# The first feed-forward layer's scale made on TensorE: its weights move past a column of silu(c)

## The chip, the cores and the metric

The kernel runs on one core of one Trainium2 chip. The metric is the time of one execution on the device in microseconds (us). A core has TensorE (PE in the rows; PEld is its weight load), VectorE (DVE), ScalarE (ACT), GpSimd (POOL) and SyncE (SP, which issues the DMAs).

## The reference

Two models of two layers each run one after the other on a sequence of 256 tokens of width 1024. In the first one every layer has a mixer (attention with compressed keys and values in layer 0, a state-space mixer in layer 1) and a feed-forward part, and both are modulated by a vector `c` of 1024 values:

```python
cs = silu(c)                                    # [1, 1024]
for i in range(2):
    shift, scale, gate = split(cs @ mod_mix_w[i] + mod_mix_b[i], 3)   # w: [1024, 3072]
    h = x * (1 + scale) + shift
    y = mla_mixer(h, ...) if i == 0 else s5_mixer(h, ...)
    x = layer_norm(ALPHA * x + (1 + gate) * y)
    shift, scale, gate = split(cs @ mod_ffn_w[i] + mod_ffn_b[i], 3)
    h = x * (1 + scale) + shift
    y = mlp(h, ...)
    x = layer_norm(ALPHA * x + (1 + gate) * y)
```

There are four such products with a vector, of three thirds with 1024 results each. The change concerns one of the twelve: `scale` of the feed-forward part of layer 0. The second model has no modulation.

## The kernel before

All instructions of an engine are issued in the order in which the program writes them. The weights come as *units* of 128x1024 f32 (0.5 MB), in an order that `plan()` writes out by hand and that is the list `UNITS`. SP loads a unit into one of seven buffers `raw0` to `raw6` as soon as the unit seven places earlier is through. A unit of kind "w" is a matrix weight: ScalarE rounds it to f32r (`wh`, L464) and VectorE makes the remainder (`wl`, L504); both are kept in a ring of 11 places. A unit of kind "p" (tiles `early`) goes to a place of its own and is used by TensorE as it is, in f32. A unit of kind "m" is a piece of a modulation. `run()` handles the next units of the list, at most so many as the call says; calls of it are strewn by hand among the instructions of a stage.

A third of a modulation is named `mod<i><third>`: i = 0 mixer of layer 0, 1 feed-forward of layer 0, 2 and 3 the same of layer 1; third 0 is shift, 1 is scale, 2 is gate. It has eight units. In each of them the weights are laid out transposed, with 128 results on the partitions and 1024 inputs along a row. `mod_unit` has VectorE multiply the tile with `cs` (silu(c), broadcast to all partitions in the setup) and sum along the row (L555: a weighted sum into one column of `msum`; the product itself goes to the scratch tile `junk`). After the eighth unit VectorE adds the bias (L564), which gives the 128x8 columns `mcol`.

In layer 0 the attention comes first. Ahead of its loop over the heads stand, in this order on TensorE: the key projection (`kvk`), the value projection (`kvv`: stationary `gate`'s storage, 128x512 results, records `bank<-early,gate`), and query pair 0 (records `bank<-gate,early`, 128x256, sixteen of them). An f32 matmul appears in the profile as two records. VectorE rotates the pair (L1227 to L1229), and the loop `heads` follows, ten rounds in the order

```python
HEADS0 = "T2 S0 B0 1 A2 E0 1 N0 q 1"
```

In round i: T turns the probabilities of head i-2 (TensorE L1094, ScalarE copy L1095), S makes the scores of head i (TensorE), B their maximum (VectorE L1284), A attends for head i-2 (TensorE `bank<-z,z`, then ScalarE and VectorE split the result into `hh` and `hl`, L636 and L637), E is the exponential (ScalarE L1289), N the normalisation (VectorE L1295, ScalarE L1298), q in rounds 0, 2 and 4 the next query pair, and each 1 is a `run` of one unit. The units of `mod11` (the third in question) are taken in this stretch: units 0 and 1 ahead of query pair 0 (one before the value projection, one after it), 2 and 3 in round 0, 4 and 5 in round 1, 6 and 7 in round 2; with one "w" unit of the output projection in each round. The gate's third `mod02` follows in rounds 3 to 6, on VectorE. After the loop `need_mod("mod02")` makes the gate's rows (TensorE `bank<-ident,gcol`), and the output projection (`mla_o`, records `bank<-wh,hh`) begins.

GpSimd computes tables for the state-space mixer during the whole loop. PSUM has eight banks, handed out and returned in a queue (`bank()`, `rel()`).

Of the kernel before, what the change touches and what calls it, by code (L numbers as in the profile page):

```python
# [11 lines left out]
F32 = mybir.dt.float32  # L12
F32R = mybir.dt.float32r
I32 = mybir.dt.int32
AF = mybir.ActivationFunctionType
OP = mybir.AluOpType
# [34 lines left out]
    return [("w", tag, k) for k in range(n)]  # L51


def _mod(i, third):
    return [("m", "mod%d%d" % (i, third), k) for k in range(8)]


def _ffn_order(tag, nt, first, pair):
# [64 lines left out]
def _unit(inp, kind, tag, k, out):  # L123
# [3 lines left out]
    def col(w):  # L127
        out[:] = w[:, 128 * k:128 * k + 128].reshape(8, 128, 128).transpose(1, 0, 2).reshape(128, 1024)

    if kind == "m":  # L130
        i, third = int(tag[3]), int(tag[4])
        nm, l = _MOD[i]
        o = 1024 * third + 128 * k
        out[:] = inp[nm + "_w"][l][:, o:o + 128].T
        return
    if tag[:3] in _FFN:
        nm, l = _FFN[tag[:3]]
# [58 lines left out]


def _cols_spec():
    s = [("dsk", lambda i: i["ssm_d"][0])]
    for m, (nm, l) in _MOD.items():  # L200
        s.append(("modb%d" % m, lambda i, nm=nm, l=l: i[nm + "_b"][l]))
    for nm in ("ln_mix", "ln_ffn"):
        for l in range(2):
            for gb in "gb":
                key = "%s_%s" % (nm, gb)
                s.append((key + str(l), lambda i, key=key, l=l: i[key][l]))
    s.append(("qn", lambda i: i["mla_q_norm"][0]))
    s.append(("kn", lambda i: i["mla_kv_norm"][0]))
    for l in range(2):
        s.append(("b1%d" % l, lambda i, l=l: i["mlp_b1"][l]))  # L210
    s.append(("bglu", lambda i: i["ssm_b_glu"][0]))
    s.append(("lbin", lambda i: i["lru_b_in_2"][0]))
    for t in range(4):
        s.append(("cw%d" % t, lambda i, t=t: i["lru_conv_w_2"][0][t]))
    s.append(("cb", lambda i: i["lru_conv_b_2"][0]))
    s.append(("lbr", lambda i: i["lru_b_r_2"][0]))
    s.append(("lbi", lambda i: i["lru_b_i_2"][0]))
    s.append(("lam", lambda i: i["lru_lambda_2"][0]))
    s.append(("cb2", lambda i: i["lru_lambda_2"][0]))
    return s  # L220
# [17 lines left out]
UNITS = plan()  # L238
# [4 lines left out]
WPOS, RPOS = [0], [0]  # L243
for _u in UNITS:
    WPOS.append(WPOS[-1] + (_u[0] == "w"))
    RPOS.append(RPOS[-1] + (_u[0] in "mwx"))
RUNITS = [_j for _j, _u in enumerate(UNITS) if _u[0] in "mwx"]
SPARE = [(WPOS[UNITS.index(("w", "ssm_in", 7)) + 1] + _k) % RING for _k in SPARES]
PUNITS = [("p", "mla_in", _k) for _k in range(4)] + [("p", "kvk", 0), ("p", "kvv", 0)] + [("p", "qb", _k) for _k in range(4)]

# [62 lines left out]
class Model:  # L313
    def __init__(self, ctx, tc, ws, cols, rows, x, pos, inv, rel, sp, sbc, sgb, out):
# [31 lines left out]
        self.cs = T("cs", [128, 1024])  # L346
        self.msum, self.gcol = T("msum", [128, 8]), T("gcol", [128, 8])
        self.mhalf = T("mhalf", [128, 4])
        self.one = T("one", [128, 1])
        self.lri = T("lri", [128, 8], I32)  # L350
        self.banks = [ps.tile([128, 512], F32, name="bank%d" % i) for i in range(8)]
# [79 lines left out]
    def run(self, look=LOOK, maxn=99, mods=2):  # L431
        n = 0
        while self.nproc < len(UNITS) and n < maxn:
            i = self.nproc
            u = UNITS[i]
            if WPOS[i] > WPOS[self.ntake] + look:
                break
            if u[0] == "m":
                if mods == 0 or (self.hold and self.modfin is not None and u[1][4] == '2'):
                    break  # L440
                mods -= 1
# [6 lines left out]
            if u[0] == "w":  # L448
                nw = self.nw
                while self.rt and nw % RING in SPARE:  # L450
                    nw += 1
                s = nw % RING
                own = self.slot_owner[s]
                if own is not None and own not in self.finished:
                    break
                if own is None and not self.lent.get(s, set()) <= self.finished:
                    break
                if self.Hs[s] is None:
                    self.Hs[s], self.Ls[s] = (self.sb.tile([128, 1024], F32R, name="w%s%d_%d" % (c, s, i), tag="w%s%d" % (c, s))
                                              for c in "hl")  # L460
                self.nw = nw + 1
                self.slot_owner[s] = u
                self.slot_of[u] = s
                self.nc.scalar.activation(self.Hs[s], raw, func=AF.Copy)  # L464
                if u[1:] in POOLED:
                    for q in range(4):
                        w = slice(256 * q, 256 * q + 256)
                        self.nc.gpsimd.tensor_tensor(self.Ls[s][:, w], raw[:, w], self.f32(self.Hs[s])[:, w], op=OP.subtract)  # L468
                else:
                    self.plo.append((raw, s))  # L470
                    if not self.lag:
                        self.rests()
            elif u[0] == "m":
                self.mod_unit(u, raw)
            elif u[0] == "x":
                self.kept[u] = raw
            self.nproc += 1
# [67 lines left out]
    def mod_unit(self, u, raw):  # L545
# [16 lines left out]
        if k == 7:  # L562
# [3 lines left out]
            else:  # L566
                nc.vector.tensor_tensor(self.gcol, self.msum, self.col("modb%d" % i, 16, 8), op=OP.add)
                nc.vector.tensor_scalar(self.gcol, self.gcol, 1.0, None, op0=OP.add)
                self.modfin = [tag, 3]

    def mod_finish(self):
        if self.modfin is None:
            return
        self.mods.add(self.modfin[0])
        self.modfin = None
        for n in range(2):
            b = self.bank()
            for m in range(4):
# [403 lines left out]
    def setup(self):  # L982
# [28 lines left out]
        for n in range(2):  # L1011
            t = self.Z[0][:, 1024 + 512 * n:1536 + 512 * n]
            nc.scalar.activation(t, cb[n], func=AF.Tanh)
            V.scalar_tensor_tensor(self.cs[:, 512 * n:512 * n + 512], t, 1.0, cb[n], op0=OP.add, op1=OP.mult)
        self.rel(*cb)
        self.ssm_decay(spt, pi)
        posf = self.posf = self.stat(2)
        V.tensor_copy(posf, posi)
# [1092 lines left out]
```

## Time and profile before

| | us |
|---|---|
| median of 3 runs | 1686.18 (1681.76 to 1689.4) |
| profiled execution | 1684.43 |
| its span | 1682.7 |
| TensorE busy in the span | 1586.5 |
| VectorE busy in the span | 1129.5 |

The span is the time from the first to the last instruction of the profiled execution; the execution's own time is 1.7 us longer. A busy time counts an engine as busy while an instruction of it is recorded; TensorE's weight loads are counted apart. The granted clock (PEclk) is the share of its full speed that TensorE was given in a stretch.

### The profile page before, as it was taken

The numbers are of one execution on the slowest core, as the hardware profiler recorded it, in microseconds if no ns is written. First come the engines' busy times: TensorE is split into PE (matmuls) and PEld (weight loads), VectorE is DVE, ScalarE is ACT, GpSimd is POOL, SyncE is SP. The second block draws the span as 40 slices with busy tenths as digits, with TensorE's granted clock in tenths as the row PEclk, the third lists the DMA queues.
The fourth block names the chain that finished last, engine by engine and source line by source line (L and its number), as shares of the span: only waits on it lengthen the run. The fifth ranks groups of instructions, "written<-read, shape, count | busy, mean of one in ns | idle before, by whom it ended". The sixth has DMA issues, their size and how long they took to land.

```text
span 1682.7 us, 24904 instructions
## 1 busy us (share of the span) xinstructions
PE 1586.5 (94%) x9594; PEld 1398.7 (83%) x9594; DVE 1129.5 (67%) x1568; ACT 841.1 (50%) x1287; POOL 237.7 (14%) x309
## 2 busy tenths in 40 slices
PE   5879989998789999999999999999999999999998
PEld 2558888987778899789997779999899998779997
DVE  7877897779977755776554876555755555675553
ACT  3454567746355655354444855443644444664441
POOL 7990000013523000100000020000000001330000
PEclk9879999998889999999999999999999999999999
DMA  9774788968466565375551747564555653545540
GB/s 360 295 251 166 256 302 288 341 231 298 163 225 247 213 226 197 141 259 205 192 176 46 245 143 252 175 238 162 210 177 180 226 199 107 179 165 202 196 151 26
DMA packets 106586, 349.62 MB, mean 208 GB/s; under 512 B 12385, under 2 KB 22753, under 8 KB 106466
## 3 DMA queue, kind: packets, MB, share of 16 engines
q1 hardware_dynamic: 106466, 348.02, 59.1%
q8 instruction: 75, 1.23, 0.3%
q14 instruction: 45, 0.37, 0.1%
HBM read 338.41 MB, written 9.57 MB: 207 GB/s over the span
## 4 chain that ended last, share of the span: by engine, by line
PE 49%; DVE 4%; ACT 3%; issue 1%; POOL 1%; DMA 0%; DVEq 0%; POOLq 0%; ACTq 0%
PE bank L400 48%; ACT junka L693 1%; DVE wl L504 1%; PE bank L644 1%; ACT wh L464 0%; DMA raw<-in_ws_dram 0%; DVE r L731 0%; POOL wl L468 0%; DVE z L1844 0%; POOL st L689 0%; DVE z L1300 0%; DVE z L1910 0%; ACT r L1870 0%; DVE st L1284 0%; ACT z L1871 0%
## 5 line engine op out<-in xcount | busy, mean ns | idle before, releaser
L504 DVE TENSOR_TENSOR wl<-raw,wh 128x1024 fp32r<-128x1024 f32 x448 | 540.1, 1240 | 163.3 <-ACT wh L464 157.7
L464 ACT ACTIVATE wh<-raw 128x1024 fp32r<-128x1024 f32 x464 | 471.5, 1051 | 246.1 <-PE bank L400 141.9
L400 PE MATMUL bank<-xh,wh 128*128 128x256 f32 x1664 | 469.1, 282 | 0.0
L400 PE MATMUL bank<-xh,wl 128*128 128x256 f32 x1664 | 468.3, 281 | 0.0
L400 PE MATMUL bank<-xl,wh 128*128 128x256 f32 x1664 | 468.1, 281 | 0.0
L400 PEld LDWEIGHTS bank<-xh,wh 128*128 128x128 f32 x1664 | 317.0, 190 | 2.7 <-DVE z L1651 0.2
L400 PEld LDWEIGHTS bank<-xl,wh 128*128 128x128 f32 x1664 | 317.0, 190 | 2.1
L400 PEld LDWEIGHTS bank<-xh,wl 128*128 128x128 f32 x1664 | 316.9, 190 | 0.0
L400 PE MATMUL bank<-wh,hh 128*128 128x512 f32 x736 | 294.7, 400 | 4.3 <-ACT hh L636 4.3
L400 PE MATMUL bank<-wl,hh 128*128 128x512 f32 x736 | 291.4, 396 | 0.0
L400 PE MATMUL bank<-wh,hl 128*128 128x512 f32 x736 | 243.2, 396 | 7.9 <-DVE hl L637 4.3
L400 PEld LDWEIGHTS bank<-wh,hl 128*128 128x128 f32 x736 | 139.8, 190 | 40.8 <-DVE hl L637 4.9
L400 PEld LDWEIGHTS bank<-wh,hh 128*128 128x128 f32 x736 | 140.6, 191 | 35.1 <-ACT hh L636 5.9
L400 PEld LDWEIGHTS bank<-wl,hh 128*128 128x128 f32 x736 | 140.4, 191 | 28.5
L555 DVE SCALAR_TENSOR_TENSOR junk<-raw,cs 128x1024 bf16<-128x1024 f32 x96 | 129.3, 1347 | 4.2 <-DMA raw<-in_ws_dram 2.9
L689 POOL TENSOR_TENSOR st<-st,mhalf 128x1 f32<-128x1 f32 (+1 forms) x33 | 22.9, 693 | 747.5 <-DVE st L697 678.9
L400 PE MATMUL bank<-wl,xh 128*128 128x512 f32 x320 | 125.9, 393 | 2.2 <-DVE wl L504 1.3
L400 PE MATMUL bank<-wh,xh 128*128 128x512 f32 x320 | 126.2, 395 | 0.7 <-ACT wh L464 0.7
L637 DVE TENSOR_TENSOR hl<-z,hh 128x512 fp32r<-128x512 f32 x68 | 47.0, 692 | 95.9 <-ACT hh L636 95.9
L400 PE MATMUL bank<-wh,xl 128*128 128x512 f32 x320 | 100.8, 392 | 2.0 <-DVE xl L637 2.0
L636 ACT ACTIVATE hh<-z 128x512 fp32r<-128x512 f32 x68 | 43.0, 633 | 104.4 <-DVE z L929 103.3
L468 POOL TENSOR_TENSOR wl<-raw,wh 128x256 fp32r<-128x256 f32 x64 | 60.7, 980 | 127.7 <-ACT wh L464 127.5
(380 smaller groups left out, 1683.3 us busy)
## 6 DMA issues: line engine op xcount, KB each, us to landing
raw<-in_ws_dram SPq DMA_DIRECT2D x580, 512.0 KB
early<-in_ws_dram SPq DMA_DIRECT2D x10, 512.0 KB
grow<-in_rows_dram SPq DMA_DIRECT2D x9, 512.0 KB
brow<-in_rows_dram SPq DMA_DIRECT2D x6, 512.0 KB
ophh<-ops_d SPq DMA_DIRECT2D x6, 512.0 KB
ophl<-ops_d SPq DMA_DIRECT2D x6, 512.0 KB
gate<-in_rows_dram SPq DMA_DIRECT2D x5, 512.0 KB
tab_d<-rot SPq DMA_DIRECT2D x4, 512.0 KB
```

The lines of the kernel that those rows point to most:

```text
L400: self.nc.tensor.matmul(out, l, r, start=start, stop=stop)
L464: self.nc.scalar.activation(self.Hs[s], raw, func=AF.Copy)
L468: self.nc.gpsimd.tensor_tensor(self.Ls[s][:, w], raw[:, w], self.f32(self.Hs[s])[:, w], op=OP.subtract)
L504: self.nc.vector.tensor_tensor(self.Ls[s], raw, self.f32(self.Hs[s]), op=OP.subtract)
L555: nc.vector.scalar_tensor_tensor(self.junk, raw, 1.0, self.cs, op0=OP.mult, op1=OP.mult, accum_out=total)
L636: self.nc.scalar.activation(hdst, src, func=AF.Copy)
L637: self.nc.vector.tensor_tensor(ldst, src, self.f32(hdst), op=OP.subtract)
L644: self.nc.tensor.transpose(b[:, 128 * j:128 * j + 128], src[:, 128 * k:128 * k + 128], self.ident)
L689: self.nc.gpsimd.tensor_tensor(r, v, self.mhalf[:, 0:n], op=OP.pow)
L693: self.nc.scalar.activation(self.junka[:, 0:512], src, func=AF.Square, scale=scale, accum_out=s[:, n:n + 1])
```

## The change

The units of `mod11` become units of kind "g". Their weights lie untransposed: 128 inputs on the partitions, 1024 results along a row. `mod_pass` has TensorE multiply them: stationary is one column of `cc` (silu(c) with 128 values in each of eight columns, made in the setup), moving are the two halves of the raw tile, and the two sums of 1x512 gather over the eight units in one partition of two PSUM banks. After the eighth unit ScalarE copies each half of the sums to `mrow` (one partition of `junk`'s storage), TensorE turns each half into four columns of a third bank by matmuls with a single one, and VectorE adds the bias to the 128x8 columns. `mod_pass` and `mod_finish` also have a path for a gate (`wide`), which isn't used: `PEMODS` holds `mod11` alone.

```diff
+PEMODS = ("mod11",)
 def _mod(i, third):
-    return [("m", "mod%d%d" % (i, third), k) for k in range(8)]
+    t = "mod%d%d" % (i, third)
+    return [("g" if t in PEMODS else "m", t, k) for k in range(8)]
...
+    if kind == "g":
+        nm, l = _MOD[int(tag[3])]
+        o = 1024 * int(tag[4])
+        out[:] = inp[nm + "_w"][l][128 * k:128 * k + 128, o:o + 1024]
+        return
...
+        self.cc, self.mrow, self.gacc = T("cc", [128, 8]), self.junk[0:1, :].bitcast(F32), {}
...
+            elif u[0] == "g":
+                self.mod_pass(u, raw)
...
+    def mod_pass(self, u, raw):
+        nc, tag, k = self.nc, u[1], u[2]
+        i, third = int(tag[3]), int(tag[4])
+        wide = third == 2
+        if k == 0:
...
+            self.gacc[tag] = [self.bank(), self.bank()]
+        acc = self.gacc[tag]
+        c = self.cc[:, k:k + 1]
...
+        for n in range(2):
+            self.mm(acc[n] if wide else acc[n][0:1, :], c, raw[:, 512 * n:512 * n + 512], k == 0, not wide and k == 7)
+        if k < 7:
+            return
...
+        b = self.bank()
+        for n in range(2):
+            nc.scalar.activation(self.mrow, acc[n][0:1, :], func=AF.Copy)
+            for m in range(4):
+                self.mm(b[:, 4 * n + m:4 * n + m + 1], self.mrow[:, 128 * m:128 * m + 128], self.one[0:1, 0:1], True, True)
+        nc.vector.tensor_tensor(self.mcol[i][third], b[:, 0:8], self.col("modb%d" % i, 8 * third, 8), op=OP.add)
+        self.mods.add(tag)
+        self.rel(b, *self.gacc.pop(tag))
...
+        cc = self.col("c", 0, 8)
+        nc.scalar.activation(self.cc, cc, func=AF.Tanh, scale=0.5)
+        V.scalar_tensor_tensor(self.cc, self.cc, 1.0, cc, op0=OP.add, op1=OP.mult)
+        V.tensor_scalar(self.cc, self.cc, 0.5, None, op0=OP.mult)
```

## Rows read from the trace of the kernel before

**Rows 1.** The page: an engine's busy us, share of the span, instructions.
```profile
PE 1586.5 (94%) x9594; PEld 1398.7 (83%) x9594; DVE 1129.5 (67%) x1568; ACT 841.1 (50%) x1287; POOL 237.7 (14%) x309
```

**Rows 2.** Busy time by stretch: PE, PEld, DVE, ACT, POOL, granted clock, DMA share, GB/s.
```profile
40.00:60.00 20.00, 16.01 (x52) 10.71 (x50) 17.52 (x39) 8.69 (x24) 18.55 (x21) 0.83 1.02 406
60.00:80.00 20.00, 15.20 (x66) 11.44 (x67) 14.04 (x30) 10.66 (x26) 18.63 (x31) 0.91 0.67 236
80.00:100.00 20.00, 16.14 (x72) 11.88 (x71) 17.20 (x27) 7.92 (x20) 19.37 (x13) 0.83 0.53 179
...
64.00:66.00 2.00, 2.00 (x11) 1.77 (x10) 1.54 (x4) 1.58 (x2) 1.80 (x7) 1.00 0.05 20
```

**Rows 3.** Timeline of TensorE: start, us, instruction; in brackets the idle time before.
```profile
52.22 3.60 PE L400 MATMUL bank<-early,gate 128*128 128x512 f32 x8
55.66 3.62 PE L400 MATMUL bank<-gate,early 128*128 128x256 f32 x16
...
61.89 0.70 PE L400 MATMUL bank<-brow,z 64*128 64x256 f32 x2 [2.19 <-DVE z L1229]
...
74.51 1.34 PE L400 MATMUL bank<-z,z 128*128 128x256 f32 x4 [2.91 <-ACT z L1095]
75.64 4.90 PE L400 MATMUL bank<-gate,early 128*128 128x256 f32 x16
80.37 0.49 PE L1094 MATMUL bank<-ident,z 128*128 128x128 f32 x3
...
82.78 0.87 PE L400 MATMUL bank<-z,z 128*128 128x256 f32 x4
...
89.90 1.65 PE L400 MATMUL bank<-z,z 128*128 128x256 f32 x4 [3.85 <-ACT z L1095]
91.35 5.57 PE L400 MATMUL bank<-gate,early 128*128 128x256 f32 x16
...
121.79 0.77 PE L400 MATMUL bank<-wh,hh 128*128 128x512 f32 x1
...
122.94 0.39 PE L400 MATMUL bank<-wl,hh 128*128 128x512 f32 x1
```

**Rows 4.** Timeline of VectorE, 58 to 101 us.
```profile
58.48 2.17 DVE L555 SCALAR_TENSOR_TENSOR junk<-raw,cs 128x1024 bf16<-128x1024 f32 x1
...
60.58 0.41 DVE L1227 TENSOR_TENSOR z<-bank,brow 128x256 f32<-128x256 f32 x1
...
86.09 0.61 DVE L1284 TENSOR_REDUCE st<-bank 128x1 f32<-128x256 f32 x2
...
96.95 0.42 DVE L1227 TENSOR_TENSOR z<-bank,brow 128x256 f32<-128x256 f32 x1 [2.12 <-PE bank L400]
...
100.36 0.62 DVE L1284 TENSOR_REDUCE st<-bank 128x1 f32<-128x256 f32 x2
```

**Rows 5.** Groups of VectorE, 56 to 86 us: count, busy us, mean ns, idle before.
```profile
L555 DVE SCALAR_TENSOR_TENSOR junk<-raw,cs 128x1024 bf16<-128x1024 f32 x8 | 12.6, 1574 | 0.1
```

**Rows 6.** Timeline of TensorE, its first matmuls.
```profile
2.52 3.75 PE L400 MATMUL bank<-grow,z 1*128 1x512 f32 x4 [2.52 <-DMA grow<-in_rows_dram]
```

**Rows 7.** Timeline of ScalarE, a copy of 512 columns out of PSUM.
```profile
48.18 0.60 ACT L1194 ACTIVATE r<-bank 128x512 f32<-128x512 f32 x1 [1.65 <-PE bank L400]
```

**Rows 8.** Waits of TensorE, 118 to 330 us: us in total, times, longest.
```profile
PE bank L400 <- DVE hl L637: 4.3, 1, 4.3
PE bank L400 <- ACT hh L636: 2.4, 2, 1.4
PE bank L400 <- ACT z L1452: 1.7, 3, 1.2
```

**Rows 9.** DMAs issued between 40.3 and 62 us.
```profile
raw<-in_ws_dram SPq DMA_DIRECT2D x9, 512.0 KB
early<-in_ws_dram SPq DMA_DIRECT2D x3, 512.0 KB
```

**Rows 10.** Timeline of VectorE soon after the setup.
```profile
13.52 1.23 DVE L555 SCALAR_TENSOR_TENSOR junk<-raw,cs 128x1024 bf16<-128x1024 f32 x1 [1.42 <-DMA raw<-in_ws_dram]
```

More of the change, by code (lines that the diff above doesn't have):

```diff
@@ L198, in _cols_spec @@
 def _cols_spec():
-    s = [("dsk", lambda i: i["ssm_d"][0])]
+    s = [("dsk", lambda i: i["ssm_d"][0]), ("c", lambda i: i["c"][0])]
     for m, (nm, l) in _MOD.items():
@@ L245 @@
     WPOS.append(WPOS[-1] + (_u[0] == "w"))
-    RPOS.append(RPOS[-1] + (_u[0] in "mwx"))
-RUNITS = [_j for _j, _u in enumerate(UNITS) if _u[0] in "mwx"]
+    RPOS.append(RPOS[-1] + (_u[0] in "gmwx"))
+RUNITS = [_j for _j, _u in enumerate(UNITS) if _u[0] in "gmwx"]
 SPARE = [(WPOS[UNITS.index(("w", "ssm_in", 7)) + 1] + _k) % RING for _k in SPARES]
@@ L437, in run @@
                 break
-            if u[0] == "m":
+            if u[0] in "gm":
                 if mods == 0 or (self.hold and self.modfin is not None and u[1][4] == '2'):
@@ L569, in mod_unit @@
                 self.modfin = [tag, 3]
+    def mod_pass(self, u, raw):
[3 more added lines that the diff above has]
+        if k == 0:
+            if wide:
+                self.mod_finish()
+            self.gacc[tag] = [self.bank(), self.bank()]
+        acc = self.gacc[tag]
+        c = self.cc[:, k:k + 1]
+        if wide:
+            c = c.to_broadcast([128, 128])
+        for n in range(2):
+            self.mm(acc[n] if wide else acc[n][0:1, :], c, raw[:, 512 * n:512 * n + 512], k == 0, not wide and k == 7)
+        if k < 7:
+            return
+        if wide:
+            self.modfin = [tag, 3]
+            return
+        b = self.bank()
[6 more added lines that the diff above has]
+        self.rel(b, *self.gacc.pop(tag))
     def mod_finish(self):
@@ L573, in mod_finish @@
             return
-        self.mods.add(self.modfin[0])
+        tag = self.modfin[0]
+        self.mods.add(tag)
         self.modfin = None
+        if tag in self.gacc:
+            acc = self.gacc.pop(tag)
+            for n in range(2):
+                for m in range(4):
+                    g = self.col("modb%s" % tag[3], 16 + 4 * n + m)
+                    self.mm(acc[n][:, 128 * m:128 * m + 128], g.to_broadcast([128, 128]), self.ident, False, m == 3)
+                self.nc.scalar.activation(self.GATE[:, 512 * n:512 * n + 512], acc[n], func=AF.Identity, bias=self.one)
+            self.rel(*acc)
+            return
         for n in range(2):
```

## The prediction

> **What bounds the kernel now.** I read the page first: TensorE is busy for 94% of the span and VectorE for 67% [rows 1]. Such averages decide nothing here, because the change sits in the attention of the first layer, so the next view was the busy time by stretch. Between 40 and 100 us the picture is another: TensorE works only 15 to 16 us of each 20 at a granted clock of 0.83 to 0.91, and VectorE 14 to 17.5 of 20 [rows 2]. Neither engine is saturated; they take turns.
>
> Which of them is late is read from the two timelines. TensorE stands still three times around the units in question: 2.19 us until VectorE has rotated the first query pair, and 2.91 and 3.85 us for ScalarE's copy of a turned probability tile [rows 3]. VectorE waits 2.12 us for the matmuls of query pair 3 (at 96.95), and otherwise mostly goes from one instruction to the next [rows 4]. At the place where the units end the order is this: TensorE has issued the scores of head 3 and goes on to an attend at 82.78 [rows 3], and VectorE takes their maximum only at 86.09 [rows 4]. So VectorE is 3.3 us behind TensorE there, and sets the pace. The eight units that the change moves are the eight weight sums of this stretch, 12.6 us with the pressure of GpSimd in it [rows 5]. From 118 us on TensorE runs almost without a gap for 100 us [rows 8]; what the heads' loop loses or gains goes into that.
>
> **The change part by part.** *VectorE loses* eight weighted sums, 8 x 1.57 = 12.6 us [rows 5], and their accumulator reads; the final addition of the bias stays. Two stand ahead of the heads' loop (the second at 58.48 [rows 4]), two in each of its rounds 0, 1 and 2.
>
> *TensorE gains* sixteen matmuls, two per unit: one column of `cc` stationary, 128x512 of the raw tile moving, in f32. No row has a one-column stationary. The nearest is the value projection, f32 with 512 moving columns: eight records in 3.60 us for four matmuls, so 0.45 us a record and 0.90 us a matmul at full clock [rows 3]. That the other operand's width matters little is seen in the broadcast of c, with one row in the array: four records in 3.75 us for two matmuls, 0.94 each, in a stretch of slow clock right after the start [rows 6]; half speed, the same columns. I take 16 x 0.90 = 14.4 us. Below, the price would be that of an f32r matmul of the output projection with as many columns, 0.39 us in one record [rows 3]; above, 1.88 us at the lower clock.
>
> The Trainium skill (TensorE: Matmul & The Clock Gate, Back-to-back issue gap) puts a sustained stream of weight loads and matmuls with 512 columns at 131 ns each. With four such passes to an f32 matmul I would estimate 0.52 us and 8.4 us in all, against 14.4. The value projection is such a stream and took 0.90 [rows 3], so the row decides. By the skill's price the change would cost 0.8 us in the end, a case of the first rival.
>
> *The end of the unit* is new: ScalarE copies 512 sums out of one partition (0.60 us for a 512-wide copy [rows 7]), TensorE turns them with four one-column matmuls, and both are done twice, the second copy waiting for the first four because there is one `mrow`. Four f32 matmuls are eight records; three turns of 128 columns took 0.49 us with the last one's drain [rows 3], so I put a record at 0.14. With 0.25 for the two handovers, an allowance, 2 x (0.60 + 0.25 + 8 x 0.14) = 4.0 us, in which TensorE does nothing else, since the turn of head 1 is queued behind them. Bounds 2.5 and 5.5. On ScalarE the copy of that turned head is queued behind `mrow`, on VectorE the maximum of head 3 behind the bias addition; both need TensorE first anyway.
>
> *Taken together for TensorE*, from 52.22 to the turn of head 1 (80.37 before): added 14.4 + 4.0 = 18.4. Given back: the wait of 2.19 shrinks to about 0.8, as VectorE's rotation (60.58 to 61.89) starts at once when the pair is there, 1.4 back; the wait of 2.91 goes, because the probabilities are long ready when TensorE comes; and no clock is lost after it, query pair 2 falling from 4.90 to 3.62 and the attend ahead of it from 1.34 to 0.87 [rows 3], 1.8 together. 18.4 - 1.4 - 2.9 - 1.8 = 12.3. The turn of head 1 comes at 92.7, and the scores of head 3 end 2.4 later at 95.1. VectorE, idle by then, takes the maximum at 95.1 instead of 86.09: 9.0 late. Its 3.3 us of arrears are what hid the rest.
>
> *What comes back after that.* From there the units on VectorE are those of before. Between the maxima of heads 3 and 5 lie 14.3 us (86.09 to 100.36), in which VectorE's sums and subtractions are stretched by GpSimd, as 58.48 shows with 2.17 us for a sum [rows 4] that takes 1.23 elsewhere [rows 10], and in which it waits 2.12 for query pair 3, slow at 5.57 after TensorE's 3.85 of idle [rows 3]. With VectorE off the shared ports in 56 to 86, GpSimd should be through its wide operations by then, and TensorE, late itself, won't idle so long. Between nothing and 4.2 us (2.1 of stretch, 2.1 of wait) I take the middle, 2.1.
>
> The Trainium skill (SBUF — State Buffer, SBUF: two separate sides) says that a VectorE operation with two SBUF inputs and a GpSimd operation exclude each other for a whole instruction. The 2.17 against 1.23 us agrees [rows 4, 10].
>
> So 9.0 - 2.1 = 6.9 us later at the end of the heads. In terms of the price p of one matmul: 16p + 4.0 - 6.1 - 3.3 - 2.1 = 16p - 7.5, which is nothing at p = 0.47 us.
>
> *Edits costed at nothing.* Silu of the column of c: three instructions of 0.2 us in the setup; VectorE soon after waits 1.42 us for a DMA [rows 10]; uncovered 0.4. The raw tiles are as many and as large as before, and SP's order is the same. TensorE wants the first tile at 52.22 and the second at about 57.5, where VectorE took the second at 58.48 and the first some 2 us before that. The first is the first of the twelve tiles of 0.52 MB issued between 40.3 and 62 us [rows 9], 15.5 us of transfer at 406 GB/s; the engines are all but still from 64 us on [rows 2], so it lands near 49 or 50 and the second a little over one us later. If they came only when VectorE took them, the value projection would wait about 4 us. Buffers of the last units come free up to 5 us later, but the tiles that reuse them are wanted 12 us after that. Two PSUM banks are held for three rounds, six circulate; a bank comes round after six allocations, over a round later; without that cover a matmul would wait for one 0.6 us copy. `mrow` lies in the scratch that VectorE's sums write; the next sum stands behind the maximum of head 3, which is later than the last read.
>
> *Does it reach the end?* From 118 us to 330 TensorE waits 8.4 us in all, 4.3 of it for one VectorE operation [rows 8], whose own chain starts from TensorE's results. I find nothing there that keeps its old time, so all 6.9 us pass on: 1684.43 + 6.9 = 1691.3 for the profiled execution. The median of the runs stands 1.75 above it, so 1693.
>
> **The rivals.** First, *not slower*: the matmuls are cheaper than any f32 row, p at or below 0.47. For it speaks that only one column of the array works; against it both f32 rows with 512 columns [rows 3, 6]. At 0.39 it gives -1.3, 1685, and up to 0.47 nothing, 1686. By the Trainium skill's sustained price (TensorE: Matmul & The Clock Gate, Back-to-back issue gap) it would be 1687. Second, *slower by more*: the 4 us of tiny matmuls and handovers let the clock fall. Before, the idle 3.85 us was followed by an attend at 1.65 for 0.87 and a query pair at 5.57 for 3.62 [rows 3]; here the scores of head 3 would take 2.4 longer, and the 2.1 not come back. With that or late tiles +9.5 to +14, 1696 to 1700; all sixteen at the lower clock would be far above. Third, *the loss doesn't reach the end*: the later wait of 4.3 us turns out to be VectorE's own and absorbs it, +2.6, 1689; against it, that VectorE there is fed by TensorE.
>
> **How the numbers follow.** The forecast (+3 to +11, so 1689 to 1697 on its own) 0.55, the cheap matmuls 0.14, the slower clock or late tiles 0.24, absorption 0.07. The range from 1685 to 1701 takes in all of these but a little at both ends, and the runs' own scatter. Half a per cent is 8.4 us, about what a measurement can tell, as the three runs shown lie within 7.6. Slower than that: most of the second rival and a quarter of the forecast, 0.35. Faster than that would need a price below nothing; 0.04 for what I have not seen. Within it 0.61.
>
> **What would show it.** In the profile after: sixteen matmuls with `cc` at 0.9 us for two records; no sums on VectorE between the first query pair and head 3; the turn of head 1 near 92.7, the maximum of head 3 near 95, the first output-projection matmul near 128.7 instead of 121.8 [rows 3]; TensorE at full clock from 52 to 88. Records of 0.25 us or a maximum of head 3 at 86 would make it wrong, and so would an output projection that starts no later than before.

## The result and the profile after

The changed kernel takes 1694.22 us (median of 8 runs, 1690.45 to 1697.38), the one before 1686.79 on the same chip: ratio 1.0051 [1.0036, 1.0066], 7.4 us slower by the medians (6.1 to 11.1 by the interval) where 6.9 were forecast. A second set of 6 runs of the same kernel (`again`, below) gave 1.0058 [1.0041, 1.0074], 9.1 us (6.9 to 12.5).

The two profiled executions lie further apart than the medians: 1697.38 is 3.2 us above the median of its kernel, and 1684.43 was 2.4 below that of its own. So 5.5 of the 13 us between their ends are scatter of single executions. What one event in one profile shows is read with that in mind throughout.

The page of the kernel after, its span and the engines' row:
```profile
span 1695.6 us, 24987 instructions
...
PE 1603.8 (95%) x9642; PEld 1410.7 (83%) x9642; DVE 1116.9 (66%) x1554; ACT 841.9 (50%) x1290; POOL 229.3 (14%) x309
```
TensorE has 17.3 us more of work and VectorE 12.6 less [rows 1]. By stretch (busy time of PE, PEld, DVE, ACT, POOL, then granted clock, DMA share, GB/s) the kernel after shows:
```profile
40.00:60.00 20.00, 16.24 (x46) 7.85 (x45) 14.13 (x36) 8.32 (x23) 17.27 (x20) 0.91 0.96 378
60.00:80.00 20.00, 18.99 (x71) 9.82 (x71) 6.87 (x14) 7.46 (x17) 18.20 (x38) 1.00 0.50 184
80.00:100.00 20.00, 19.27 (x86) 12.13 (x84) 6.67 (x17) 8.09 (x21) 19.13 (x41) 0.91 0.48 164
```
Against [rows 2], VectorE's 14 and 17.2 us of 20 have become 7, and TensorE's 15 and 16 have become 19, at a higher clock. Two engines that took turns are now one that works and one that waits for it. The new work in TensorE's groups between 40 and 132 us (count, busy us, mean ns, idle before):
```profile
L410 PE MATMUL bank<-raw,cc 128*1 128x512 f32 x32 | 14.9, 591 | 0.0
...
L410 PE MATMUL bank<-one,junk 1*128 1x1 f32 x16 | 2.1, 248 | 0.7 <-ACT junk L605 0.7
```
Its timeline at the places that the prediction named, with the lines that answer to [rows 3]:
```profile
54.33 3.70 PE L410 MATMUL bank<-early,gate 128*128 128x512 f32 x8
...
64.93 0.70 PE L410 MATMUL bank<-brow,z 64*128 64x256 f32 x2 [1.01 <-DVE z L1284]
...
88.30 1.88 PE L410 MATMUL bank<-raw,cc 128*1 128x512 f32 x4
90.11 1.05 PE L410 MATMUL bank<-one,junk 1*128 1x1 f32 x8
91.89 1.05 PE L410 MATMUL bank<-one,junk 1*128 1x1 f32 x8 [0.73 <-ACT junk L605]
92.87 0.55 PE L1149 MATMUL bank<-ident,z 128*128 128x128 f32 x3
...
95.75 1.60 PE L410 MATMUL bank<-z,z 128*128 128x256 f32 x4
...
129.41 0.48 PE L410 MATMUL bank<-wh,hh 128*128 128x512 f32 x1
```
The wait ahead of the first query pair's scores has shrunk from 2.19 to 1.01 us, the last unit's matmuls start at 88.30, the end of the unit takes until the turn of head 1 at 92.87, and the first output projection comes at 129.41 instead of 121.79. VectorE's timeline shows who waits for whom there:
```profile
82.29 0.62 DVE L1339 TENSOR_REDUCE st<-bank 128x1 f32<-128x256 f32 x2 [2.17 <-PE bank L410]
...
92.97 0.17 DVE L608 TENSOR_TENSOR mc<-bank,cols 128x8 f32<-128x8 f32 x1 [2.22 <-PE bank L410]
95.99 0.62 DVE L1339 TENSOR_REDUCE st<-bank 128x1 f32<-128x256 f32 x2 [2.85 <-PE bank L410]
...
108.58 0.61 DVE L1339 TENSOR_REDUCE st<-bank 128x1 f32<-128x256 f32 x2
```
In [rows 4] the maximum of head 3 stood at 86.09 and waited for nobody. Now VectorE has stood 2.85 us when the scores arrive at 95.99. And TensorE's waits from 118 to 340 us:
```profile
PE bank L410 <- DVE hl L688: 5.3, 2, 4.8
PE bank L410 <- ACT z L1150: 4.6, 2, 4.0
PE bank L410 <- ACT z L1507: 2.2, 2, 1.8
```
The long wait for VectorE's `hl`, 4.3 us in [rows 8], is 4.8 here: it moved along with the rest and took nothing up.

### The profile page after: what moved, and what is told of

The parts are those of the page before. It is cut to its first block, busy times and chain, and to the rows that moved or that the text cites. A ratio compares the mean times of both kernels' runs of the same rounds, so it can differ in the third digit from the quotient of the medians.

```text
span 1695.6 us, 24987 instructions
## 1 busy us (share of the span) xinstructions
PE 1603.8 (95%) x9642; PEld 1410.7 (83%) x9642; DVE 1116.9 (66%) x1554; ACT 841.9 (50%) x1290; POOL 229.3 (14%) x309
## 4 chain that ended last, share of the span: by engine, by line
PE 49%; DVE 4%; ACT 3%; issue 1%; DMA 1%; POOL 0%; DVEq 0%; POOLq 0%; ACTq 0%
PE bank L410 48%; ACT junka L744 1%; ACT wh L474 1%; DVE wl L516 1%; PE bank L695 1%; DMA raw<-in_ws_dram 0%; POOL wl L478 0%; DVE z L1899 0%; DVE r L782 0%; DVE z L1355 0%; DVE z L1965 0%; ACT r L1925 0%; DVE st L1339 0%; ACT z L1926 0%; DMA brow<-in_rows_dram 0%
## 5 line engine op out<-in xcount | busy, mean ns | idle before, releaser
L567 DVE SCALAR_TENSOR_TENSOR junk<-raw,cs 128x1024 bf16<-128x1024 f32 x88 | 115.5, 1312 | 4.2 <-DMA raw<-in_ws_dram 3.0
```

The source lines that it names most:

```text
L567: nc.vector.scalar_tensor_tensor(self.junk, raw, 1.0, self.cs, op0=OP.mult, op1=OP.mult, accum_out=total)
```

## The experiments

The theory is the prediction's working: TensorE now sets the pace, and each matmul (0.93 us) and the end of the unit (4 us forecast, 2.8 in the profile after) are on the path, less the waits of TensorE that vanish, VectorE's 3.3 us of arrears and what comes back later. The rivals: the lateness comes from something else that the edit brought (the two banks held, the place of the units, an end that holds up other work), or it is the clock's doing. Every kernel below was timed against the one before, in runs on one chip; its profile was taken once. "Stretch" goes from 52.00 us to the first output projection matmul and "idle" is that less TensorE's busy time in it, both from the windows view of one profile. As 52.00 is a fixed time, and the value projection or the unit ahead of it began anywhere between 50.2 (`weave`) and 52.9 (`f32r`), stretches compare to within some 2 us.

| kernel | median, us | before | ratio [95%] | stretch | idle | clock |
|---|---|---|---|---|---|---|
| before | | | | 69.8 | 15.8 | 0.83 |
| after | 1694.22 | 1686.79 | 1.0051 [1.0036, 1.0066] | 77.4 | 8.6 | 0.91 |
| again | 1695.14 | 1686.06 | 1.0058 [1.0041, 1.0074] | 81.6 | 7.8 | 0.85 |
| double | 1705.95 | 1686.06 | 1.0122 [1.0105, 1.0139] | 89.8 | 9.4 | 0.93 |
| drop | 1681.00 | 1686.06 | 0.9973 [0.9959, 0.9987] | 64.2 | 12.7 | 0.87 |
| late_end | 1694.61 | 1686.06 | 1.0055 [1.0038, 1.0071] | 76.7 | 7.3 | 0.89 |
| banks | 1688.40 | 1686.15 | 1.0013 [1.0002, 1.0024] | 74.3 | 17.0 | 0.75 |
| colmov | 1699.00 | 1686.15 | 1.0075 [1.0061, 1.0089] | 81.4 | 9.0 | 0.80 |
| f32r | 1700.19 | 1686.15 | 1.0087 [1.0072, 1.0102] | 82.3 | 17.3 | 0.79 |
| weave | 1693.65 | 1686.15 | 1.0040 [1.0025, 1.0056] | 72.7 | 6.6 | 0.89 |
| f32r_ahead | 1687.27 | 1687.17 | 1.0000 [0.9985, 1.0015] | 68.4 | 8.8 | 0.83 |
| half | 1688.00 | 1687.17 | 1.0008 [0.9996, 1.0020] | 71.9 | 10.0 | 0.84 |
| half_late | 1689.02 | 1687.17 | 1.0014 [1.0001, 1.0028] | 71.6 | 12.0 | 0.88 |
| f32r_late | 1681.68 | 1686.42 | 0.9976 [0.9964, 0.9988] | 67.4 | 7.0 | 0.82 |

### again: the changed kernel once more

> The changed kernel once more. Theory A (TensorE's new matmuls and the end of the unit are on the path ahead of head 3, and nothing else changed): 7 to 9 us over the kernel before, and in its profile the first matmul of the output projection about 7.6 us later than before, with the same lateness at the end of the span, give or take 3 us of scatter. Rival B (something later in the kernel suffers too, since the profiled execution was 12.9 us longer and only 7.6 of that are there at the output projection): the lateness grows past 900 us again, to 12 or 13 us.

It came out at 9.1 us over the kernel before, with an interval that overlaps most of that of the first set; theory A's 7 to 9 lies inside it. Its profile is worth more than its time, because it shows what one program scatters. One row of the windows view, 94 to 106 us, of the changed kernel and then of this one:
```profile
94.00:106.00 12.00, 11.55 (x51) 8.68 (x51) 7.83 (x18) 7.00 (x19) 11.79 (x37) 0.86 0.55 171
```
```profile
94.00:106.00 12.00, 12.00 (x36) 7.96 (x36) 6.63 (x14) 4.41 (x13) 11.75 (x38) 0.50 0.37 128
```
The same instructions in the same order: after the end of the unit the clock stayed at half for the whole stretch in one execution and recovered in the other. The first output projection came at 133.63 here and at 129.41 there, 11.8 and 7.6 us later than before; the 11.8 is more than theory A's 7.6 give or take 3. Of an event in a single profile, 4 us can be the clock's and not the kernel's.

Rival B asks whether something later in the kernel suffers too. One instruction some 430 us into the span can be found in every profile; here it is before and in `again`:
```profile
433.27 0.94 PE L1699 MATMUL bank<-ident,b2row 64*128 64x64 f32 x8 [1.52 <-ACT b2row L1689]
```
```profile
442.24 0.94 PE L1754 MATMUL bank<-ident,b2row 64*128 64x64 f32 x8 [2.74 <-ACT b2row L1744]
```
Its start, with the first output projection and the end of the span, in us (`banks` and `drop` are described below):

| profile | output projection | this instruction | end of the span |
|---|---|---|---|
| before | 121.79 | 433.27 | 1682.7 |
| after | 129.41 | 441.61 | 1695.6 |
| again | 133.63 | 442.24 | 1694.9 |
| banks | 126.25 | 434.85 | 1687.0 |
| drop | 116.16 | 428.07 | 1680.6 |

Against the one profile of before the four stand at +8.3, +9.0, +1.6 and -5.2 us there, and at +12.9, +12.2, +4.3 and -2.1 at the end. The last two kernels do no work of the new kind on TensorE and lose 2.7 and 3.1 us in that later part all the same, `again` 3.2 and the profile after 4.6. So most of the later growth belongs to the one profile of before and not to the change, and rival B is not borne out. The other reading is as useful: of the 4.2 us by which `again` lay behind the profile after at the output projection, 0.6 were left at 430 us. Most of what this one profile lost there was made up by then.

### double: every unit's matmuls twice

```
+        for r in range(2):
+            for n in range(2):
+                self.mm(acc[n][0:1, :], c, raw[...], k == 0 and r == 0, k == 7 and r == 1)
...
-        V.tensor_scalar(self.cc, self.cc, 0.5, None, op0=OP.mult)
+        V.tensor_scalar(self.cc, self.cc, 0.25, None, op0=OP.mult)
```


> Every matmul of the unit is issued twice, with the column of silu(c) halved, so the sums stay what they are. Theory A (TensorE sets the pace from the value projection to the scores of head 3, and a matmul costs it 0.92 us): 14 to 15 us more than the changed kernel, so 21 to 24 over the kernel before. Rival C (the matmuls fill time in which TensorE would wait anyway, and the loss comes from the end of the unit and the banks that are held): 7 to 10 over before, as the changed kernel.

It is 19.9 us over the kernel before, 10.8 to 12.5 more than the changed kernel (by its two sets). Its group of matmuls and its stretch from 52 to 124 us:
```profile
L410 PE MATMUL bank<-raw,cc 128*1 128x512 f32 x64 | 28.6, 592 | 0.0
```
```profile
52.00:124.00 72.00, 67.98 (x254) 33.00 (x253) 28.22 (x56) 26.54 (x65) 49.48 (x117) 1.00 0.49 173
```
Theory A's 21 to 24 is just missed by the medians and lies within the interval (17.7 to 23.4); rival C's 7 to 10 does not. 13.7 us of matmuls were added, and between eight and nine tenths of them arrive at the end. So TensorE's work is on the path, at a little under its own length. What fits the remainder is the clock: it is 1.00 through all 72 us here, with the same small matmuls of the end in them (from 103.27), where the changed kernel lost it behind them. That the added work kept it up is not shown apart from this.

### drop: the third left out

```
             elif u[0] == "g":
-                self.mod_pass(u, raw)
+                if u[2] == 7:
+                    self.nc.vector.tensor_copy(self.mcol[1][1], self.col("modb1", 8, 8))
+                    self.mods.add(u[1])
```
The tiles are still loaded; no engine multiplies them, and the third is its bias alone.

> The third is left out on both engines: the units are loaded, nothing is multiplied, and the bias alone stands in for the result. Theory A, by its own formula with the matmuls' price and the end at nothing, gives 11.5 us less than before; with VectorE and the chain over the engines limiting sooner, 8 to 12 less. Rival D (VectorE's sums were no more on the path before than TensorE's matmuls are now, so that the stretch waits for something else, ScalarE or GpSimd): within 3 us of before.

Only 5.1 us faster than before (2.2 to 6.9 by the interval), which lies between theory A's 8 to 12 and rival D's 3, though VectorE is rid of 12.6 us and TensorE of everything new. The prediction's sum, with nothing for matmuls and end, would give -11.5; its slope does not hold downwards. Two rows of the windows view and TensorE's waits from 50 to 117 us say why:
```profile
60.00:80.00 20.00, 17.95 (x81) 13.13 (x81) 9.22 (x19) 11.06 (x27) 18.22 (x37) 0.91 0.65 247
...
100.00:120.00 20.00, 15.38 (x65) 12.17 (x64) 10.86 (x25) 12.04 (x26) 17.47 (x61) 0.76 0.89 299
```
```profile
PE bank L410 <- ACT z L1152: 10.9, 5, 4.0
PE bank L410 <- DVE z L1286: 1.7, 1, 1.7
```
Without the eight sums TensorE still waits 10.9 us for ScalarE's copies of turned probabilities, and the clock is still below 1. What is left looks like the chain of a head over three engines: scores, maximum, exponential, turn, copy, attend; how much of it is that chain and how much the clock is not separated. Left out, the third was worth about 5 us to the kernel before, and no placing of it below won more than that. It is no strict bound, as the added work on TensorE in `double` went with a higher clock.

### late_end: the end spread over the gate's first two units

```
+        for q in range(4):
+            nc.scalar.activation(self.mrow[q], acc[q // 2][0:1, 256 * (q % 2):256 * (q % 2) + 256], func=AF.Copy)
...
+        if tag == "mod02" and k == 0:
+            self.mod_turn()      # the eight small matmuls
+        if tag == "mod02" and k == 1:
+            self.mod_add()       # the bias
```


> Only the end of the unit is changed: the sums are copied to four pieces of free rows at once, so that TensorE waits for no copy, and its eight small matmuls stand after the scores of head 3, the bias addition one sum later. Theory A (the end holds up the turn of head 1 by 4.0 us, of which about 2.1 are matmuls that now delay the attend of head 1 only): 2 to 3.5 us less than the changed kernel, 4 to 6 over before. Rival C (the handovers at the end are the loss): no more than 1 us over before. Rival E (the chain over ScalarE and VectorE in that round hides the end): as the changed kernel, 7 to 9 over before.

8.6 us over the kernel before, between the two sets of the changed kernel (7.4 and 9.1): nothing gained. Theory A's 4 to 6 is missed and rival E's 7 to 9 met, though not for its reason, since the end was not hidden in its round. The timeline of TensorE shows that the edit did its part:
```profile
89.29 0.55 PE L1161 MATMUL bank<-ident,z 128*128 128x128 f32 x3
...
98.22 1.60 PE L410 MATMUL bank<-z,z 128*128 128x256 f32 x4
99.61 4.76 PE L410 MATMUL bank<-gate,early 128*128 128x256 f32 x16
```
The turn of head 1 comes at 89.29, 3.6 us earlier than in the profile after, and the maximum of head 3 at 91.95, 4.0 earlier. Then the small matmuls, now at 91.84 to 93.7, are followed, a round later, by a slow attend (1.60 us for 0.87) and a slow query pair (4.76 for 3.62): the clock is 0.72 from 94 to 106 us. The first output projection stands at 128.72. Most of what was won at head 3 had gone by the end of the heads.

### banks: the old sums, and two banks held

```
-PEMODS = ("mod11",)
+PEMODS = ()
...
+        if tag == "mod11" and k == 0:
+            self.gacc[tag] = [self.bank(), self.bank()]
+        if tag == "mod11" and k == 7:
+            b = self.bank()
+            self.rel(b, *self.gacc.pop(tag))
```


> The sums stay on VectorE as before; of the change there are only the silu of the column in the setup and the two PSUM banks held from the first unit to the last. Theory A: within 1.5 us of the kernel before. Rival C (six circulating banks make the heads' loop wait): 3 to 7 us over before.

2.2 us over, with an interval from 0.3 to 4.0, so between theory A's 1.5 and rival C's 3. From 46 to 126 us TensorE waits for no bank, only for ScalarE's copies (13.6 us, as much as in the kernel before) and VectorE's rotation, 3.4. After that wait the timeline reads:
```profile
61.23 0.86 PE L410 MATMUL bank<-brow,z 64*128 64x256 f32 x2 [3.44 <-DVE z L1289]
...
63.59 6.08 PE L410 MATMUL bank<-gate,early 128*128 128x256 f32 x16
```
The query pair took 6.08 us where it takes 3.62 at full clock: the clock again. So the holding of the banks, with the column's silu in the setup, explains at most 4 of the changed kernel's 7.4 to 9.1 us. No wait shows a cost of it, and at 430 us this profile is only 1.6 us behind (above); but the interval leaves out zero, and where the 2.2 us come from is not shown.

### colmov: the weights stationary, the column moving

```
-        for n in range(2):
-            self.mm(acc[n][0:1, :], c, raw[:, 512 * n:512 * n + 512], k == 0, k == 7)
+        for m in range(8):
+            self.mm(acc[0][:, m:m + 1], raw[:, 128 * m:128 * m + 128], c, k == 0 and m == 0, k == 7 and m == 7)
```
The sums then arrive as columns, and the end needs neither copies nor small matmuls.

> The other way round: the weights are stationary, 128x128 at a time, and the column of silu(c) moves, so that the 1024 results stand on the partitions and the end of the unit with its copies falls away; 64 f32 matmuls of one column in place of 16 of 512. Theory A with the price of a record between the 0.13 us that the one-column matmuls at the end of the unit took and the 0.19 us of a full weight load: 128 records, 16.6 to 24 us on TensorE against 18.9 now, so 5 to 13 us over before. Rival F (the price goes by the moving columns alone, so one column is next to nothing): 5 to 10 us less than before.

12.9 us over, 4 to 5 worse than the changed kernel and at the upper end of theory A's 5 to 13. Its reason was another, though: at full clock the records cost 0.115 us each, 14.7 in all, below the 16.6 that the theory began with, and the end is gone. The timeline shows a unit at 1.84 us for sixteen records of one column, against 1.88 for the four records of 512 columns, and what then happens:
```profile
65.20 2.18 PE L410 MATMUL bank<-cc,raw 128*128 128x1 f32 x16
67.24 5.10 PE L410 MATMUL bank<-gate,early 128*128 128x256 f32 x16
72.17 1.84 PE L410 MATMUL bank<-cc,raw 128*128 128x1 f32 x16
...
86.40 3.52 PE L410 MATMUL bank<-cc,raw 128*128 128x1 f32 x16
```
```profile
64.00:88.00 24.00, 24.00 (x119) 20.03 (x117) 7.09 (x13) 7.47 (x17) 22.28 (x34) 0.70 0.42 133
```
TensorE is busy in all 24 us from 64 to 88, and the granted clock is 0.70: it falls behind the unit at 65.20, and the query pair behind that takes 5.10 us for 3.62. The order of the operands changes nothing in the price of a unit at full clock; it goes with a lower clock in what follows. What fills the time is different. TensorE's groups of weight loads from 40 to 140 us, of this kernel and of the changed one, are:
```profile
L410 PEld LDWEIGHTS bank<-cc,raw 128*128 128x128 f32 x128 | 19.5, 238 | 0.6 <-issue 0.5
```
```profile
L410 PEld LDWEIGHTS bank<-raw,cc 128*1 128x1 f32 x32 | 2.1, 82 | 8.0 <-issue 7.8
```
Here every one-column matmul brings a load of 128 columns, and the loads are busy for 19.5 us, as long as the matmuls (19.2); in the changed kernel they are 2.1 beside 14.9.

### f32r, f32r_ahead, f32r_late: cheaper matmuls

In these three both operands are rounded to f32r, the weights by a copy on ScalarE, so the products are no longer those of the kernel before. `f32r` rounds each tile right before its matmuls:
```
+        nc.scalar.activation(self.grnd[k % 2], raw, func=AF.Copy)
+        raw = self.grnd[k % 2]
```


> ScalarE rounds each unit's tile to f32r (1.05 us each) and TensorE multiplies the rounded tile with a rounded column in one pass; the result is less exact than f32. Theory A (the price of the matmul decides; 0.24 us in place of 0.92, 16 x 0.24 = 3.8 us instead of 14.9): 3.7 us less than before by its formula, with ScalarE's eight roundings in a round's chain between 4 less and 1 more. Rival C: 7 to 9 over before, as the changed kernel. Rival G (a one-column stationary has a floor of its own): in between, with records well above 0.24 us.

Every expectation missed: 14.0 us over. The matmuls did become cheap, and TensorE stood for ScalarE instead, as its group from 40 to 140 us and the windows view of 70 to 88 show:
```profile
L410 PE MATMUL bank<-g,cc 128*1 128x512 f32 x16 | 6.4, 492 | 9.3 <-ACT g L596 9.3
```
```profile
70.00:88.00 18.00, 12.70 (x36) 6.96 (x37) 5.25 (x10) 7.68 (x15) 17.21 (x16) 0.56 0.48 175
```
9.3 us of waiting in order, in five waits of up to 3.45, and a clock of 0.56 behind them. `f32r_ahead` rounds the same tiles on the same engine, but multiplies the tile of the unit before:
```
+        for j in ([k - 1] if k else []) + ([7] if k == 7 else []):
+            for n in range(2):
+                self.mm(acc[n][0:1, :], self.cc[:, j:j + 1], self.grnd[j % 2][:, 512 * n:512 * n + 512], j == 0, j == 7)
```


> As f32r, except that ScalarE rounds a tile one unit ahead: TensorE's two f32r matmuls of a unit read the tile that was rounded in the unit before, and only the last of the eight reads its own. The roundings (1.1 us each on ScalarE) are still there. Theory A (f32r lost its time to TensorE standing in order behind ScalarE's roundings, 1.75, 1.63, 2.23 and 3.45 us, and to the clock that fell in those waits; the matmuls themselves are cheap at 0.24 us from start to start): without the waits the units cost TensorE 16 x 0.31 = 5 us in place of 14.4, so by the prediction's sum between 2 us faster and 3 slower than before. Rival (ScalarE's work or f32r with a one-column stationary is itself what costs): 10 to 15 us slower than before, as f32r. Second rival, out of the run with the third left out (only 4.6 us faster, with the clock down to 0.8): TensorE with so little work loses its clock, and the result lies between, 4 to 9 slower.

Level with the kernel before, 1.0000 [0.9985, 1.0015], as the first theory said. The same view:
```profile
L410 PE MATMUL bank<-g,cc 128*1 128x512 f32 x16 | 5.8, 445 | 1.2 <-ACT g L598 1.2
```
ScalarE's work is unchanged, the waits went from 9.3 to 1.2 us and the loss from 14.0 to 0.1. So it was the order of waiting, with the clock behind it, not ScalarE's time or the one-column f32r matmul. The turn of head 1 is at 82.44 here, still behind the end of the unit. `f32r_late` spreads that end over the gate's first three units:
```
+        if tag == "mod02" and k == 0:
+            self.mod_copy()      # the last two matmuls, ScalarE's four copies
+        if tag == "mod02" and k == 1:
+            self.mod_turn()      # the eight small matmuls
+        if tag == "mod02" and k == 2:
+            self.mod_add()       # the bias
```


> As f32r_ahead, and the end of the unit is spread over the gate's first three units: the last two f32r matmuls and ScalarE's four copies at the first, the eight small matmuls at the second, the bias addition at the third, so that nothing of it is waited for. Theory A (in f32r_ahead the end still held the turn of head 1 for 3.8 us, from 78.61 to 82.44, and the clock fell to 0.62 after it; those are on the path): 3 to 5 us faster than before, about as much as the run with the whole third left out (4.6). Rival (as in late_end, where the end made earlier gave nothing: what is won at the maximum of head 3 goes to the later attends and to the clock): between 1.5 us faster and 1.5 slower than before.

4.7 us faster than before by the medians, ratio 0.9976 [0.9964, 0.9988], about as much as leaving the third out (5.1), as theory A said. TensorE's and VectorE's timelines around head 3:
```profile
78.90 0.49 PE L1175 MATMUL bank<-ident,z 128*128 128x128 f32 x3
...
81.27 0.65 PE L410 MATMUL bank<-g,cc 128*1 128x512 f32 x2
```
```profile
80.56 2.06 DVE L516 TENSOR_TENSOR wl<-raw,wh 128x1024 fp32r<-128x1024 f32 x1
82.55 0.61 DVE L1365 TENSOR_REDUCE st<-bank 128x1 f32<-128x256 f32 x2
```
The scores end at about 81.5, the maximum at 82.55 follows VectorE's own work without a wait: VectorE is 1.1 us behind TensorE there, where it was 3.3 before and TensorE was the late one after the change. (Its one profiled execution, 1685.38, is 3.7 us above its median; the time is taken from the twelve runs.) Why spreading the end pays here and not in `late_end` is not shown. In `late_end` VectorE stood 1.90 us for the scores of head 3, so TensorE was still the late one; that fits, but the clock of the two profiles differs as well.

### weave: the eight units by turns with the gate's

```
-    m, w = _mod(1, 0) + _mod(1, 1) + _mod(0, 2), _w("mla_o", 8)
+    m, w = _mod(1, 0) + [u for p in zip(_mod(1, 1), _mod(0, 2)) for u in p], _w("mla_o", 8)
```


> Only the order of the units is changed: a unit on TensorE and a unit of the gate on VectorE take turns, one of each per round, so that the matmuls stand where TensorE waits for the turned probabilities ahead of each attend, and VectorE has one sum a round through seven rounds in place of none in three and two in four. Theory A (what counts is which engine is late in a round): less lost than in the changed kernel, 2 to 6 over before. Rival H (the total of TensorE's work in the stretch decides, wherever it stands): 7 to 9 over before. Rival I (the two engines balanced make up for all of it): 1 to 4 less than before.

7.5 us over, no better than the changed kernel beyond the intervals: rival H's 7 to 9 is met, but the interval, 4.2 to 9.4, reaches into theory A's 2 to 6. The end now stands at the end of the heads' loop and is 1.3 us dearer, since TensorE waits for both copies:
```profile
104.81 1.05 PE L410 MATMUL bank<-one,junk 1*128 1x1 f32 x8 [1.33 <-ACT junk L605]
106.60 1.05 PE L410 MATMUL bank<-one,junk 1*128 1x1 f32 x8 [0.73 <-ACT junk L605]
```
Its profiled execution is the fastest of its eleven (1686.17), and its first unit started 1.8 us ahead of 52.00, so its 72.7 us of stretch in the table flatters it.

### half and half_late: 512 results on each engine

Both load the other 512 columns as four units of 256 inputs, two f32 matmuls each:
```
+        for e in range(2):
+            self.mm(acc[0][0:1, :], self.cc[:, 2 * k + e:2 * k + e + 1], raw[:, 512 * e:512 * e + 512], k == 0 and e == 0, k == 3 and e == 1)
...
+    m, w = _mod(1, 0) + [u for k in range(4) for u in (("g", "mod11", k), ("m", "mod11", k))] + _mod(0, 2), _w("mla_o", 8)
```
`half_late` has the gate's third ahead of these eight units.

> Only half of the third goes to TensorE: 512 of its 1024 results, in four units of 256 inputs (two f32 matmuls each, one accumulation bank), by turns with four weighted sums on VectorE for the other 512; the end is one copy and four small matmuls. Theory A (the cost is the sum of the prediction: TensorE's matmuls at 0.93 each less VectorE's arrears of 3.3 us and the waits that vanish): 8 x 0.93 + 2.0 - 6.1 - 3.3 - 2.1 = -2, so from 2 us faster to 1.5 slower than before. Rival (out of the run with double the matmuls, where 14.9 us of matmuls cost 10.8: each matmul costs about 0.7 of itself however few there are): 4 to 6 us slower than before. Second rival (TensorE has to wait in order for the later tiles of its half): 6 us slower or more.

> As half, but the units of the gate's third come first and the eight half units after them, in the rounds of the heads 3 to 6, where TensorE of the kernel before waits up to 3.85 us ahead of the attends. Theory A (TensorE's matmuls are free where TensorE waits for VectorE's sums; the sums are what the pace is set by there): 1 to 4 us faster than before. Rival (the pace there is set by the clock after each wait, and the time comes back slower wherever the matmuls stand): 2 to 5 us slower than before.

`half` is 0.8 us over, inside what the sum gave (-2 to +1.5) and below the proportional rival. `half_late` is 1.9 over, just under its rival's 2 to 5 and against the theory. In `half_late` TensorE waits only 0.84 us from 86 to 108, where the matmuls now stand, but the early waits are there in full:
```profile
61.38 1.01 PE L411 MATMUL bank<-brow,z 64*128 64x256 f32 x2 [3.44 <-DVE z L1289]
...
77.52 0.89 PE L411 MATMUL bank<-z,z 128*128 128x256 f32 x4 [3.22 <-ACT z L1155]
```
The gate's sums are now the ones that VectorE makes ahead of those waits. The intervals of the two overlap, so which order is better is not settled.

## Why the prediction was right, point by point

**The matmul.** Forecast 0.90 us, measured 0.93 (14.9 us for sixteen). The row of the value projection [rows 3] was the right neighbour: an array with one column in use is no cheaper. The first rival, p at 0.47 or below, was false for f32. The other support was weaker than it read: 0.94 us in [rows 6] is a record and not a matmul, and that it was a record at half speed is not in the trace, which gives a clock of 1.00 for that time:
```profile
0.00:20.00 20.00, 11.19 (x28) 6.04 (x28) 11.90 (x33) 4.97 (x14) 14.94 (x16) 1.00 0.84 306
```

**The end of the unit.** Forecast 4.0 us, measured 2.8 (90.11, the first small matmul, to the turn at 92.87). The working had the first copy wait for all sixteen matmuls; ScalarE's copies need one accumulator each, and only the second was waited for, 0.73 us.

**Given back.** The wait for the rotation shrank by 1.2 (forecast 1.4); the one for the copy of the first turned head went (2.9); query pair 2 took 3.62 and the attend ahead of it 0.92, which is 1.7 back (forecast 1.8); the clock was 1.00 from 60 to 80 us. So 17.7 added less 5.8 is 11.9, with 0.3 from a later start (52.52 for 52.22) 12.2, and the turn of head 1 was 12.5 late; the last 0.3 are not traced to one place. The forecast had 12.3 out of 18.4 less 6.1. That it came within 0.2 is partly luck: the end was put 1.2 too high, the matmuls 0.5 too low, what is given back 0.3 too high, and 0.6 had no term.

**The maximum of head 3.** Forecast 95.1, measured 95.99: the scores slowed at their end, and the attend behind them took 1.60. This much of the second rival, the clock behind the small matmuls, is real, and `again` shows it at its worst, half clock for 12 us. Of the 0.9 us at this place 0.2 came with the turn of head 1 and 0.7 with the slow scores; in the other execution it was more. The small matmuls alone do not bring it about: in `double` the clock stayed at 1.00 behind them.

**What came back.** Forecast 2.1; from head 3 to head 5 it took 12.6 us for 14.3, so 1.7 were recovered. The output projection was 7.6 us late in the profile after (forecast 6.9), 11.8 in that of `again`. The medians, 7.4 and 9.1, lie 0.5 and 2.2 above the forecast; 6.9 is inside the first interval and at the edge of the second, so a forecast that was too low is not shown beyond the noise. If it was, the clock behind the end of the unit is the likely place.

**It reaches the end.** The 4.3 us wait for `hl` moved and absorbed nothing; the third rival was false.

**Costed at nothing.** No wait of TensorE for a tile or a bank is seen in the heads, in the profile after or in `banks`. The time of `banks`, 2.2 us over, leaves open whether that was worth nothing.

**The slope.** 16p - 7.5 says 21.1 for `double` (p = 1.79) and 19.9 were measured; -1.7 for `f32r_ahead` (p = 0.36), measured +0.1; -2 for `half`, measured +0.8. It fails for `drop`: -11.5, measured -5.1. The sum has one engine's arrears in it and takes them as given back without limit. No run here went below about -5; there something else limits, the chain over the engines or the clock. The reading of who is late was also incomplete. The prediction names one wait of VectorE, 2.12 us at 96.95; the timeline of the kernel before has another, longer one among the units in question:
```profile
80.57 0.42 DVE L1227 TENSOR_TENSOR z<-bank,brow 128x256 f32<-128x256 f32 x1 [2.38 <-PE bank L400]
```
There VectorE stood for query pair 2. So TensorE was the late one 5.5 us ahead of the maximum of head 3, and VectorE's 3.3 us of arrears at 86.09 arose behind that point. This fits `drop`, where 12.6 us fewer of sums won 5.1.

In one sum, by the table: the changed kernel's TensorE is busy 14.8 us longer in the stretch (68.8 for 54.0) and idle 7.2 less (8.6 for 15.8), 7.6 in all. Half of the new work went into idle time, the other half into the span.

## What to carry to other kernels

Where two engines take turns, work moved from one to the other is paid at the receiver's price less what the receiver had been waiting, and the gain on the giver is limited by what remains: leave the work out altogether first, and its time tells what a placing can hope for (here 5 us, of 12.6 that the sums took; the best placing tried won 4.7). A cheaper form of the work helps only if nothing that it needs is waited for in order: the same rounding cost 14 us one unit too late and nothing one unit ahead. And a new operation's end, a handful of tiny matmuls between two copies, can lose more in the clock behind it than by its own length, and not in every run.

## What the runs showed of the hardware that was not expected

- An f32 matmul costs as much with a one-column stationary and 512 moving columns (1.88 us for the two of a unit) as the same sums do with the weights stationary and one moving column (1.84 us for the eight of a unit). In the second form the weight loads are busy as long as the matmuls (19.5 and 19.2 us), in the first hardly (2.1 and 14.9).
- With one-column matmuls between them TensorE was busy in all of 64 to 88 us, and the granted clock was 0.70, so the lower of the two levels for much of it; with twice the 512-column matmuls it was 1.00 from 52 to 124 us, with 4 us of waits in it.
- The same program kept the half clock for 12 us after the small matmuls in one execution (0.50) and not in another (0.86), which moved the first output projection by 4.2 us; at 430 us 0.6 of it were left.
- An f32 matmul with 128 stationary columns on one partition and a single moving value takes two records of 0.13 us from start to start, eight records in 1.05 us.
